# Queries of a hybrid decoder layer: projected in slabs by dimension, rotated in rows and sent through DRAM, instead of by item of four heads

## The chip, the cores and the metric

The kernel runs on one core of a Trainium2 chip. The metric is the time of one execution in microseconds (us) on the device. TensorE (PE in the profile, PEld its weight loads) does the matmuls; VectorE (DVE), ScalarE (ACT) and GpSimd (POOL) work element by element; SyncE (SP) issues all DMAs of this kernel. SBUF is the memory on the chip, with 128 partitions; matmul results arrive in PSUM, which has eight banks of 512 f32 a partition.

## What is computed

One decoder layer over 2048 tokens of width 1024, f32 in and out:

```python
h = rmsnorm(x, attn_norm)
z = h @ w_in              # [pool 1024 | q 16 heads x 64 | k, v 2 heads x 64 | two gates 1024 each]
q = partial_rope(rmsnorm(q, q_norm), positions) * 64 ** -0.5    # per head; the first 16 of 64 dimensions turn
k = partial_rope(rmsnorm(k, k_norm), positions)
b = swa_sink_attention(q, k, v, sinks)      # window of 128 tokens, 8 query heads to one key head
a = pool_mixer(u_pool)                      # causal means over 2, 4, 8, 16 tokens, a matrix a group
x = x + (g_pool * a + g_attn * b) @ w_out
h = rmsnorm(x, ffn_norm)
up = causal_depthwise_conv(h @ w_up)        # 2 x 2816 wide, 3 taps
x = x + (silu(gate) * val) @ w_down
```

`partial_rope` turns dimension d of the first eight with dimension d + 8: `x1 cos - x2 sin` and `x2 cos + x1 sin`. The norm divides by one number a head and token, so it can be applied after the scores' product: the kernel puts it into the scale of the exponential.

## The kernel before

It works through two chunks of 1024 tokens. Each chunk runs a mixer (projections, attention, pooling, gates), the output projection, the up projection and the down projection; the mixers are 0 to about 510 us and 1254 to about 1710 us of the profile. Each f32 operand is kept as a high and a low half in a reduced f32 format (fp32r), and a product is three matmuls: high by high, high by low, low by high. `mm3` issues them, so all projections have its line (L221 before, L225 after).

The program is written with a framework that allots tiles from pools of rotating buffers and fixes, before the run, one order of instructions for each engine; at run time each engine goes through its list in that order and waits on semaphores. So does SyncE with the DMAs, all of which `load` issues (L199 before, L203 after): a DMA that waits for its data holds up those behind it. PSUM tiles have the tags f, a and t, of two banks each, and s, one tile of two banks. SBUF tiles have tags too: U (the large ones), M, Q, R, F, and small ones.

A mixer starts with eight blocks of 128 tokens, in which keys and values are made (`keys_values`). Then come 32 items: four groups of four heads (q4 = 3, 2, 1, 0), and within each the eight blocks n of 128 tokens. An item before is:

- `queries` of the next item: 24 matmuls of 256 columns (four heads) into bank a; sums of squares in `head_rstd` (a ScalarE square, a VectorE reduction L649, an addition, a power on GpSimd L651); the rotation in `rope` (L629 to L633); and the high and low halves into a tile Q (casts L716, L718 on ScalarE, differences L717, L719 on VectorE).
- `transposes` (L725) of these through TensorE into bank t and by ScalarE into the layout of the scores, dimensions on partitions (L727). They stand at the end of the item's last filler.
- `probabilities` of the item before: four transposes (L774), a cast, a difference (L777) and two masks on GpSimd (L780, L783).
- `scores`: eight matmuls into s (L742), the window's mask (L751), the maximum (L756), four exponentials with the norm as scale (L763), and the division by the sum (L767).
- the fillers: units of 24 matmuls of 512 columns of the gates and of the pooled channels ("ga", "pu", "pg", `filler`), which give TensorE work while the other engines do the softmax. `fillers` shares them out: 8, 12, 12 and 8 to the groups, of eight items each, so 24 items of a chunk have one filler and 8 have two (chunk 0's first group also has units that fold the pooling matrices).
- `values` of the item before: four matmuls (L796) into bank a, added into the output of the gate (L803 to L806).

`first_fillers` puts some units between the blocks of keys and values. `weight_order` is the order in which weights are loaded; in chunk 0 they are split into halves and these kept in DRAM for chunk 1 (`made_`... in the DMAs).

## Time and profile before

| | |
|---|---|
| Time, three runs | 2460.86, 2460.86, 2464.63 us; median 2460.86 |
| The profiled execution | 2466.2 us, its span 2464.0 |
| TensorE's granted clock | 0.997 of full |
| HBM | 214 MB read, 87 MB written |
| DMA queue of SyncE | 94608 packets, 34.6% of 16 engines' span |

The profile is of one execution. Busy is the time in which an engine executes; the chain that ended last is followed back from the last instruction. A group of instructions is a line, an engine, an operation and its tiles with their shapes, with the count, the busy time in us and the mean ns of one; behind the second bar stands the engine's idle time before them and what ended it. In the timeline a row is a run of like instructions, from its first start. Matmuls overlap: the next one starts before the last has ended, so that the cost of a piece is the distance of two starts.

### The profile page before, as it was taken

Reading aid. Unit: us, or ns where it says so; the run is one execution under the profiler, and the core shown is the slowest. Engines: PE = TensorE matmul, PEld = TensorE weight load, DVE = VectorE, ACT = ScalarE, POOL = GpSimd, SP = SyncE. Lnnn points to the kernel's source line nnn. Section 1 sums busy time; section 2 is a strip of 40 time slices with the busy share of each in tenths; the row PEclk is TensorE's granted clock in tenths of the full one; section 3 lists DMA queues with packets and bytes.
Section 4 is the critical chain, followed back from the end, with each engine's and each line's share of the span. In section 5 each row is a group of like instructions: output and inputs, shape, how many; then the busy total and the mean of one; then the engine's idle time right before and its main releaser. Section 6 shows DMA issues by size and latency. Waiting matters only on the chain.

```text
span 2464.0 us, 32845 instructions
## 1 busy us (share of the span) xinstructions
PE 2426.2 (98%) x12224; PEld 2056.7 (83%) x12224; DVE 1928.2 (78%) x3452; ACT 1151.1 (47%) x2294; POOL 225.1 (9%) x217
## 2 busy tenths in 40 slices
PE   7999999999999999999999999999999999999999
PEld 7888888877888888888888888888888888887887
DVE  7778777877888887899846766678569888788994
ACT  6544444545555555543513443444445554554432
POOL 0122221200000000000002322222000000000000
PEclk9999999999999999999999999999999999999999
DMA  8613233257322233544332122211542222218321
GB/s 326 256 71 120 87 129 129 78 196 271 115 94 77 96 112 109 182 177 162 111 146 86 52 83 72 90 53 43 184 171 103 77 91 88 79 69 282 132 74 52
DMA packets 94767, 303.33 MB, mean 123 GB/s; under 512 B 10128, under 2 KB 12560, under 8 KB 83600
## 3 DMA queue, kind: packets, MB, share of 16 engines
q1 hardware_dynamic: 94608, 301.24, 34.6%
q8 instruction: 96, 1.57, 0.3%
q14 instruction: 63, 0.52, 0.1%
HBM read 214.17 MB, written 87.03 MB: 122 GB/s over the span
## 4 chain that ended last, share of the span: by engine, by line
PE 83%; DVE 10%; ACT 3%; issue 1%; DMA 1%; POOL 0%; SPq 0%; DVEq 0%; ACTq 0%
PE f L221 22%; PE f L1009 18%; PE t L1009 9%; PE a L221 6%; PE a L1009 4%; PE a L1299 4%; PE f L1299 4%; PE s L1299 4%; PE t L1299 4%; ACT Q L763 2%; PE s L742 1%; PE a L796 1%; DVE F L846 1%; PE t L774 1%; DVE U L206 1%
## 5 line engine op out<-in xcount | busy, mean ns | idle before, releaser
L221 PE MATMUL f<-U,U 128*128 128x512 f32 (+1 forms) x3168 | 735.8, 390 | 15.6 <-ACT U L205 8.3
L221 PEld LDWEIGHTS f<-U,U 128*128 128x128 f32 x3168 | 585.7, 190 | 136.9 <-DVE U L206 10.5
L1009 PE MATMUL f<-U,U 128*128 128x512 f32 x1512 | 359.8, 390 | 1.3 <-ACT Q L1027 1.3
L1009 PEld LDWEIGHTS f<-U,U 128*128 128x128 f32 x1512 | 283.5, 188 | 61.5 <-ACT Q L1027 2.2
L1075 DVE SCALAR_TENSOR_TENSOR M<-F,vc,M 128x1024 f32<-128x1024 f32 x176 | 225.0, 1282 | 129.3 <-ACT M L1072 129.0
L1009 PE MATMUL t<-U,U 128*128 128x512 f32 x1080 | 254.2, 389 | 0.0
L221 PE MATMUL a<-U,U 128*128 128x256 f32 x1920 | 247.1, 284 | 1.3 <-DVE M L500 1.3
L221 PEld LDWEIGHTS a<-U,U 128*128 128x128 f32 x1920 | 241.5, 192 | 6.7 <-ACT rB L567 1.5
L1009 PEld LDWEIGHTS t<-U,U 128*128 128x128 f32 x1080 | 202.8, 188 | 42.1
L763 ACT ACTIVATE Q<-s,st,r 128x128 f32<-128x128 f32 x256 | 114.2, 453 | 172.7 <-DVE st L758 166.6
L651 POOL TENSOR_TENSOR r<-r,mhalf 128x4 f32<-128x4 f32 (+1 forms) x80 | 76.4, 955 | 929.4 <-DVE r L650 897.5
L322 ACT CAST U<-R 128x1024 fp32r<-128x1024 f32 x120 | 125.5, 1053 | 65.9 <-DVE R L343 33.9
L323 DVE TENSOR_TENSOR U<-R,U 128x1024 fp32r<-128x1024 f32 x120 | 146.7, 1222 | 0.0
L1009 PE MATMUL a<-U,U 128*128 128x512 f32 x576 | 138.6, 390 | 0.0
L1009 PE MATMUL f<-U,M 128*128 128x512 f32 x504 | 124.3, 395 | 4.0 <-DVE F L1053 4.0
L1009 PEld LDWEIGHTS a<-U,U 128*128 128x128 f32 x576 | 108.0, 188 | 22.2
L1258 ACT CAST U<-U 128x1024 fp32r<-128x1024 f32 x74 | 77.2, 1051 | 86.1 <-PE a L1299 26.5
L1009 PEld LDWEIGHTS f<-U,M 128*128 128x128 f32 x504 | 95.8, 191 | 24.7 <-DVE F L1053 4.9
L1072 ACT ACTIVATE M<-F,vc 128x1024 f32<-128x1024 f32 x88 | 109.3, 1243 | 1.3
L1061 ACT COPY F<-f 128x512 f32<-128x512 f32 x42 | 24.6, 586 | 181.0 <-PE f L1009 181.0
L206 DVE TENSOR_TENSOR U<-R,U 128x512 fp32r<-128x512 f32 x142 | 93.9, 691 | 7.8 <-ACT U L205 7.2
L1259 DVE TENSOR_TENSOR U<-U,U 128x1024 fp32r<-128x1024 f32 x74 | 89.7, 1220 | 10.3 <-ACT U L1258 10.3
(259 smaller groups left out, 3892.8 us busy)
## 6 DMA issues: line engine op xcount, KB each, us to landing
R<-w_up SPq DMA_DIRECT2D x80, 512.0 KB, 3.3
actd<-M SPq DMA_DIRECT2D x44, 512.0 KB, 2.6
U<-w_down SPq DMA_DIRECT2D x88, 256.0 KB, 5.0
U<-actd SPq DMA_DIRECT2D x88, 256.0 KB, 5.2
R<-w_out SPq DMA_DIRECT2D x32, 512.0 KB, 4.7
U<-kept SPq DMA_DIRECT2D x12, 1024.0 KB, 7.5
made_ga<-U SPq DMA_DIRECT2D x8, 1024.0 KB, 7.9
made_q<-U SPq DMA_DIRECT2D x8, 1024.0 KB, 7.3
```

The source lines that it names most:

```text
L206: V.tensor_sub(lo[:, t], src[:, t], hi[:, t].bitcast(F32))
L221: nc.tensor.matmul(out, a, b, start=(i == 0), stop=(i == n - 1))
L322: A.copy(t[:, 0], raw)
L323: V.tensor_sub(t[:, 1], raw, t[:, 0].bitcast(F32))
L651: G.tensor_tensor(r, r, mhalf[:, 0:nh], op=ALU.pow)
L763: A.activation(pr[:, h, :], sc[:, h, 0:P], AF.Exp, bias=nm[:, h:h + 1], scale=it["rq"][:, h:h + 1], accum_out=rs[:, h:h + 1])
L1009: nc.tensor.matmul(bank, a[:, x, k, :], b[k // 2][:, y, k % 2, :], start=(first and i == 0), stop=(i == 11), skip_group_check=True)
L1072: A.activation(y, u[:, 2:], AF.Identity, bias=cw[:, 3, m:m + 1], scale=cw[:, 2, m:m + 1])
L1075: V.scalar_tensor_tensor(y, u[:, j:j + T], cw[:, j, m:m + 1], y, op0=ALU.mult, op1=ALU.add)
L1258: A.copy(hi, src)
L1259: V.tensor_sub(lo, src, hi.bitcast(F32))
L1299: nc.tensor.matmul(into[m], u[:, 0, c_], v[:, 1], start=(first and j == 0), stop=(k == n - 1 and j == 2), skip_group_check=True)
```

## The change

The queries are no longer made for each item but as units of the same kind as the fillers. The columns of `w_q` are reordered on the host so that a slab of 128 columns is 16 dimensions of eight heads. There are eight slabs j (0 to 3 for heads 0 to 7, 4 to 7 for heads 8 to 15), each in two halves n of 512 tokens. A unit `queries(c, j, n)` is 24 matmuls with 512 tokens moving, so that its result has dimensions and heads on partitions and tokens along the row. Even slabs go to bank f, odd ones to bank a, and behind the odd one the pair is finished: squares added; for the first pair of each eight heads, whose slabs hold the dimensions that turn together, `rotate` with sine and cosine as rows; high and low halves into tiles M; and eight writes of 64 partitions to DRAM (`qd`). The sums of squares over a head's dimensions are four f32 matmuls with a matrix of ones and zeros (`heads8`, L728). `rope_rows` makes the rows once a chunk from the tables that the keys use, by eight f32 matmuls with the identity (L491).

`load_queries` reads an item's queries from DRAM in the layout of the scores, 256 KB in one DMA, two items ahead. With that the items' `queries` and `transposes` are gone, and so are the queries' own tables.

The eight units of heads 8 to 15 stand between the blocks of keys and values (`first_fillers`), with the four "ga" units behind them; those of heads 0 to 7 are fillers of the first two groups, which have 12, 16, 12 and 8 fillers now: 16 items of a chunk have one filler and 16 have two. In an item scores come first; `probabilities` of the item before follow them, or stand behind the first filler where there are two. Tag Q has five buffers instead of four. Later lines have shifted: scores are L770, the window's mask L779, the division L795, probabilities L802 to L805, values L824.

```diff
+def queries_of(pair):
+
+    return [("q", 2 * pair + j, n) for n in range(2) for j in range(2)]
...
-    out = sum(ga[:1] + pg[:1] + fold + pu[:1] + ga[1:] + pg[1:] + pu[1:], [])
+    q = [queries_of(i)] if i < 2 else []
+    out = sum(ga[:1] + pg[:1] + q + fold + pu[:1] + ga[1:] + pg[1:] + pu[1:], [])
...
-        return [ga[0:1], [], ga[1:2], [], ga[2:3], [], ga[3:4], []]
+        return [q[0:1], q[1:2], q[2:3], q[3:4], q[4:5], q[5:6], q[6:7], q[7:8] + ga]
     fold = [("fold", j, 0) for j in FOLDS[FOLD_LEAD:FOLD_FIRST]]
-    return [[], fold[0:1], fold[1:2] + ga[0:1], fold[2:3] + ga[2:3] + fold[3:4], ga[1:2], [],
-            ga[3:4], []]
+    return [[], fold[0:1], fold[1:2] + q[0:2], fold[2:3] + fold[3:4], q[2:4], q[4:5], q[5:6],
+            q[6:8] + ga]
...
-    qp = pool("qp", 4)
+    qp = pool("qp", 5)
...
+    heads8 = cp.tile([P, 8], F32, "heads8")
+    V.reduce_sum(heads8, ident.rearrange("p (d h) -> p h d", h=8), axis=AX.X)
...
+    def rope_rows(c):
+
+        rows = up_.tile([P, 2, T], F32, "U")
+        pb = ps2.tile([P, T], F32, "s")
+        rb = mp.tile([P, NB, P], F32, "M")
+        V.tensor_copy(rb.rearrange("p b (i d h) -> p (b i) d h", i=2, d=8),
+                      ck[:, c * NB:(c + 1) * NB].rearrange("p b i d -> p (b i) d").unsqueeze(3)
+                      .to_broadcast([P, 2 * NB, 8, 8]))
+        for n in range(NB):
+            nc.tensor.matmul(pb[:, n * P:(n + 1) * P], rb[:, n, :], ident, start=True, stop=True)
+        for i in range(2):
+            A.copy(rows[0:64, i], pb[64 * i:64 * i + 64])
+        return rows
...
-    def queries(it):
+
+
+
+    qd = [[dp.tile([2, HD, 8, 512], F32, f"qd_{i}_{n}") for n in range(2)] for i in range(2)]
+    rq = cp.tile([P, 2, NB, 8], F32, "rq")
+    STARTS = ((0, 16), (8, 24), (32, 40), (48, 56))
+
+    def queries(c, j, n, hs, ta, st):
+        if n == 0:
+            st["q", j] = stream.get("q", j, later=later)
+        pq, c_ = project(hs, st["q", j], n, "fa"[j % 2])
+        sq = qp.tile([P, 512], F32, "Q")
+        A.square(sq, pq)
+        if j % 2 == 0:
+            st["even"] = pq, sq
+            return
+        pe, acc = st.pop("even")
+        V.tensor_add(acc, acc, sq)
+        if j % 4 == 1:
+            rotate(pe, pq, st["rows"], c_)
+        own, at = j // 4, j % 4
+        for i, src in ((at - 1, pe), (at, pq)):
+            t = mp.tile([P, 2, 512], F32R, "M")
+            A.copy(t[:, 0], src)
+            V.tensor_sub(t[:, 1], src, t[:, 0].bitcast(F32))
+            for e, r in enumerate(STARTS[i]):
+                load(qd[own][n][:, r:r + 8].rearrange("a d h t -> (d h) a t"),
+                     t[64 * e:64 * e + 64].bitcast(F32))
+        pn = ps.tile([P, 512], F32, "t")[:, 0:32].rearrange("p (b h) -> p b h", b=4)
+        for b in range(4):
+            nc.tensor.matmul(pn[:, b], acc[:, b * P:(b + 1) * P], heads8, start=True, stop=True)
+        r = rq[:, own, 4 * n:4 * n + 4]
+        if at == 1:
+            V.tensor_tensor(r, pn, e1[:, c, 4 * n:4 * n + 4].unsqueeze(2)
+                            .to_broadcast([P, 4, 8]), op=ALU.add)
+        else:
+            V.tensor_add(r, pn, r)
+            r = r.rearrange("p b h -> p (b h)")
+            G.tensor_tensor(r, r, mhalf, op=ALU.pow)
+
+    def rotate(a, b, rows, c_):
+
+        h = slice(0, 64)
+        c, s = rows[h, 0, c_], rows[h, 1, c_]
+        ga, gb = (vc[h, V_QG + i:V_QG + i + 1] for i in range(2))
+        t = mp.tile([P, 2, 512], F32, "M")
+        for i, (x, g) in enumerate(((a, ga), (b, gb))):
+            V.scalar_tensor_tensor(t[h, i], x[h], g, s, op0=ALU.mult, op1=ALU.mult)
+            V.scalar_tensor_tensor(x[h], x[h], g, c, op0=ALU.mult, op1=ALU.mult)
+        V.tensor_sub(a[h], a[h], t[h, 1])
+        V.tensor_add(b[h], b[h], t[h, 0])
+
+    def load_queries(it):
         c, q4, n = it["c"], it["q4"], it["n"]
-        hs, wq = it["hs"], it["wq"]
-        c_ = slice(n * P, (n + 1) * P)
-        bank = ps.tile([P, 512], F32, "a")
-        pq = bank[:, 0:256]
-        mm3(pq, [(hs[k][:, 0, c_], hs[k][:, 1, c_], wq[k // 4][:, 0, k % 4, :],
-                  wq[k // 4][:, 1, k % 4, :]) for k in range(KT)])
-        q = pq.rearrange("p (h d) -> p h d", h=4)
-        rq = head_rstd(bank, 4, c, n)
-        qr = sp.tile([P, 4, 16], F32, "qr", 1)
-        rope(qr, q, "q", c * NB + n, 4)
-        qs = qp.tile([P, 4, 2, HD], F32R, "Q")
-        A.copy(qs[:, :, 0, 16:HD], q[:, :, 16:HD])
-        V.tensor_sub(qs[:, :, 1, 16:HD], q[:, :, 16:HD], qs[:, :, 0, 16:HD].bitcast(F32))
-        A.copy(qs[:, :, 0, 0:16], qr)
-        V.tensor_sub(qs[:, :, 1, 0:16], qr, qs[:, :, 0, 0:16].bitcast(F32))
-        it.update(rq=rq, qs=qs)
-
-    def transposes(it):
-        pt = ps.tile([P, 4, P], F32R, "t")
-        for h in range(4):
-            nc.tensor.transpose(pt[:, h, :], it["qs"][:, h].rearrange("p a d -> p (a d)"), identr)
-        qT = qp.tile([P, 4, P], F32R, "Q")
-        A.copy(qT, pt.bitcast(F32))
-        it["qT"] = qT
+        it["qT"] = qp.tile([P, 4, P], F32R, "Q")
+        h, b = 4 * (q4 % 2), n % 4
+        load(it["qT"].bitcast(F32), qd[q4 // 2][n // 4][:, :, h:h + 4, b * P:(b + 1) * P]
+             .rearrange("a d h t -> (a d) h t"))
+        it["rq"] = rq[:, q4 // 2, n, h:h + 4]
...
         ta, st = {}, {}
+        if c > 0:
+            st["rows"] = rope_rows(c)
         for n in range(NB):
+            if c == 0 and n == 2:
+                st["rows"] = rope_rows(c)
...
-        wq = {3: stream.get("q", 3)}
-        items = [dict(c=c, q4=q4, n=n, hs=hs, kts=kts, vs=vs, ta=ta)
+        items = [dict(c=c, q4=q4, n=n, kts=kts, vs=vs, ta=ta)
                  for q4 in (3, 2, 1, 0) for n in range(NB)]
-        def head(i):
-            items[i]["wq"] = wq[items[i]["q4"]]
-            queries(items[i])
-
-        head(0)
-        transposes(items[0])
+        for it in items[0:2]:
+            load_queries(it)
         for i in range(len(items)):
             group, n = divmod(i, NB)
-            if n == NB - 3 and group < 3:
-                wq[2 - group] = stream.get("q", 2 - group)
-            if i + 1 < len(items):
-                head(i + 1)
-            if i > 0:
+            scores(items[i])
+            if i + 2 < len(items):
+                load_queries(items[i + 2])
+            fills = fillers(c, group)[n]
+            if i > 0 and len(fills) == 1:
                 probabilities(items[i - 1])
-            scores(items[i])
             run_later()
-            parts = fillers(c, group)[n]
-            for f in parts:
-                if f == parts[-1] and i + 1 < len(items):
-                    between.append(lambda: transposes(items[i + 1]))
+            for j, f in enumerate(fills):
+                if i > 0 and j == 1:
+                    probabilities(items[i - 1])
                 filler(*f, c, hs, ta, st)
             if i > 0:
                 values(items[i - 1])
...
-        "w_q": c(w[:, 1024:2048].reshape(2, 4, P, 4, 256).transpose(3, 0, 2, 1, 4)),
+        "w_q": slabs(w[:, 1024:2048][:, order]),
```

TensorE in the last group of chunk 1's mixer, one item; U_14668 and U_14670 are the queries' weights, U_11063 to U_11208 the normed tokens, t, a, s and f PSUM tiles. Before (the scores L742 and the filler follow):

```order
L725 MATMUL t_15712<-identr_136,Q_15643 128x128 x4
L796 MATMUL a_15721<-M_15656,U_11269 128x512 x2
L796 MATMUL a_15721<-M_15653,U_11269 128x512 x2
L221 MATMUL a_15732<-U_14668,U_11063 128x256 x3
L221 MATMUL a_15732<-U_14668,U_11085 128x256 x3
L221 MATMUL a_15732<-U_14668,U_11107 128x256 x3
L221 MATMUL a_15732<-U_14668,U_11130 128x256 x3
L221 MATMUL a_15732<-U_14670,U_11153 128x256 x3
L221 MATMUL a_15732<-U_14670,U_11170 128x256 x3
L221 MATMUL a_15732<-U_14670,U_11189 128x256 x3
L221 MATMUL a_15732<-U_14670,U_11208 128x256 x3
L774 MATMUL t_15773<-identr_136,Q_15675 128x128 x4
```

The changed kernel at the same place, up to the filler's first product and from its last one on to the next item's transposes:

```order
L824 MATMUL a_14015<-M_13984,U_10406 128x512 x2
L824 MATMUL a_14015<-M_13981,U_10406 128x512 x2
L770 MATMUL s_14026<-U_10404,Q_13896 128x256 x8
L802 MATMUL t_14052<-identr_136,Q_13966 128x128 x4
L225 MATMUL f_14067<-U_10200,U_13987 128x512 x3
```

```order
L225 MATMUL f_14067<-U_10345,U_13987 128x512 x3
L824 MATMUL a_14094<-M_14060,U_10406 128x512 x2
L824 MATMUL a_14094<-M_14057,U_10406 128x512 x2
L770 MATMUL s_14105<-U_10404,Q_13974 128x256 x8
L802 MATMUL t_14131<-identr_136,Q_14042 128x128 x4
```

The queries' products and their transposes are gone from the item, scores stand ahead of the transposes of the probabilities, and one filler is all that lies between those and the values.

VectorE at the same place; a_15721 and a_14094 are the values' bank, s the scores. Before:

```order
L806 SCALAR_TENSOR_TENSOR U_14067<-U_14067,Q_15726 128x2x128
L649 TENSOR_REDUCE r_15758<-a_15732 128x4
L629 TENSOR_TENSOR rope_15763<-a_15732,cq_181 128x64
L650 TENSOR_SCALAR r_15758<-r_15758,e_20_185 128x4
L631 TENSOR_TENSOR rope_15763<-a_15732,sq_182 128x4x8 x2
L777 TENSOR_TENSOR M_15778<-t_15773,M_15778 128x512
L633 TENSOR_TENSOR qr_15762<-rope_15763 128x64
L717 TENSOR_TENSOR Q_15768<-a_15732,Q_15768 128x4x48
L751 COPY_PREDICATED s_15784<-causal_140,s_15784 128x4x128
L719 TENSOR_TENSOR Q_15768<-qr_15762,Q_15768 128x4x16
L756 TENSOR_REDUCE st_15794<-s_15784 128x4
```

After:

```order
L832 TENSOR_TENSOR Q_14099<-a_14094,Q_14099 64x256
L779 COPY_PREDICATED s_14105<-causal_142,s_14105 128x4x128
L832 TENSOR_TENSOR Q_14099<-a_14094,Q_14099 64x256
L784 TENSOR_REDUCE st_14115<-s_14105 128x4
L834 SCALAR_TENSOR_TENSOR U_13003<-U_13003,Q_14099 128x2x128
L785 SCALAR_TENSOR_TENSOR st_14115<-st_14115,rq_193 128x4
L805 TENSOR_TENSOR M_14136<-t_14131,M_14136 128x512
L786 TENSOR_TENSOR st_14115<-st_14115,nsink_147 128x4
L905 SCALAR_TENSOR_TENSOR U_12089<-F_13750,vc_102,U_12089 128x512
```

The seven operations of the queries, six of them ahead of the window's mask, are gone, and the work on the values and the probabilities' low half now stands among that on the scores.

SyncE at the end of chunk 0's blocks of keys and values, in the changed kernel; R are raw weights, `made_` their halves kept for chunk 1, `qd` the queries in DRAM, Q an item's queries:

```order
L203 DMA qd_0_4_191<-M_1342 64x2x512 x2
L203 DMA R_1525<-w_q 128x1024
L203 DMA qd_0_4_191<-M_1347 64x2x512 x2
L203 DMA qd_1_5_192<-M_1449 64x2x512 x2
L203 DMA Q_1611<-qd_0_4_191 128x4x128
L203 DMA Q_1613<-qd_0_4_191 128x4x128
L203 DMA qd_1_5_192<-M_1454 64x2x512 x2
L203 DMA made_ga_0_13_1532<-U_1527 128x2048
```

Before, the same stretch of the queue is:

```order
L199 DMA R_1392<-w_ga 128x1024
L199 DMA made_ga_0_10_1394<-U_1269 128x2048
L199 DMA R_1630<-w_q 128x1024
L199 DMA R_1632<-w_q 128x1024
L199 DMA made_pu_0_11_1634<-U_1506 128x2048
L199 DMA R_1890<-wfold_84 128x1024
```

The query writes and the reads of the first items stand between weights and their copies; a write there waits for the difference on VectorE that ends its tile.

More of the change, by code (lines that the diff above doesn't have):

```diff
@@ L59 @@
 V_SK = V_CB + 44
-V_N = V_SK + NH
+V_QG = V_SK + NH
+V_N = V_QG + 2
 class Pool:
@@ L144, in weight_order @@
         out += [(kind, j) for parts in first_fillers(c) for kind, j, n in parts if n == 0]
-        out.append(("q", 3))
         for i in range(4):
-            for n, parts in enumerate(fillers(c, i)):
-                if n == NB - 3 and i < 3:
-                    out.append(("q", 2 - i))
-                out += [(kind, j) for kind, j, h in parts if h == 0]
+            out += [(kind, j) for parts in fillers(c, i) for kind, j, h in parts if h == 0]
         out += [("pg", ct) for ct in slabs_of(3)]
@@ L224, in block_kernel @@
     wfold = dp.tile([8, P, 8, P], F32, "wfold")
-    slabs = {"ga": w_ga, "pu": wfold, "pg": w_gp, "out": w_out, "fold": w_poolT}
+    slabs = {"ga": w_ga, "pu": wfold, "pg": w_gp, "out": w_out, "fold": w_poolT, "q": w_q}
     made = {}
@@ L241, in load_weights @@
             return None
-        if kind == "q":
-            srcs = [w_q[a[0], j] for j in range(2)]
-        elif kind == "up":
+        if kind == "up":
             srcs = [w_up[a[0]], w_up[FT + a[0]]]
@@ L270, in split_weights @@
             shape = [P, 2] + list(raw.shape)[1:]
-            if key[0] == "q":
-                out.append(up_.tile(shape, F32R, "U"))
-            else:
-                p, tag = (mp, "M") if out and key[1] not in FOLDS[:FOLD_LEAD] else (up_, "U")
-                out.append(p.tile(shape, F32R, tag))
+            p, tag = (mp, "M") if out and key[1] not in FOLDS[:FOLD_LEAD] else (up_, "U")
+            out.append(p.tile(shape, F32R, tag))
             hi, lo = out[-1][:, 0], out[-1][:, 1]
@@ L380, in block_kernel @@
     load(raw[1], w_poolT[lead[1]])
-    def load_gains():
-        t = qp.tile([P, 2, HD], F32, "Q")
-        load(t, qkn.rearrange("p (a d) -> p a d", a=2))
-        return t
-    gains = load_gains()
+    gains = qp.tile([P, 2, HD], F32, "Q")
+    load(gains, qkn.rearrange("p (a d) -> p a d", a=2))
     def load_rest():
@@ L477, in block_kernel, with rope_tables @@
     vcar = cp.tile([P, 2, P], F32R, "vcar")
-    cq = cp.tile([P, 16, 16], F32, "cq")
-    sq_ = cp.tile([P, 16, 16], F32, "sq")
     ck = cp.tile([P, 16, 2, 8], F32, "ck")
-    tabs["q"], tabs["k"] = (cq, sq_), ck
-    def rope_tables(chunk, gains):
+    tabs["k"] = ck
+    def rope_rows(c):
[10 more added lines that the diff above has]
+        return rows
+    def rope_tables(chunk):
         n, at = [P, NB, 8], slice(chunk * NB, (chunk + 1) * NB)
@@ L527, in rope_tables @@
             A.activation(dst, u, AF.Sin, scale=-tau)
-        for h in range(2):
-            own = gains[:, 0, 8 * h:8 * h + 8].unsqueeze(1).to_broadcast(n)
-            other = gains[:, 0, 8 - 8 * h:16 - 8 * h].unsqueeze(1).to_broadcast(n)
-            V.tensor_tensor(cq[:, at, 8 * h:8 * h + 8], cos, own, op=ALU.mult)
-            V.scalar_tensor_tensor(sq_[:, at, 8 * h:8 * h + 8], sin, 2.0 * h - 1.0, other,
-                                   op0=ALU.mult, op1=ALU.mult)
     r1 = cp.tile([P, NCH, NB], F32, "r1")
@@ L1339, in mixer @@
             block_b(n)
+            if n == 2 and c == 0:
+                turn(0)
             for f in fills:
                 filler(*f, c, hs, ta, st)
-            if n == 2 and c == 0:
-                turn(0)
             if n > 1 or n == c == 1:
@@ L1391, in block_kernel @@
     scaled()
-    rope_tables(0, gains)
+    rope_tables(0)
     for i, j in enumerate(FOLDS[:FOLD_LEAD]):
@@ L1433, in _layout @@
     w = np.asarray(w_in)[0]
+    starts = np.array([0, 16, 8, 24, 32, 40, 48, 56]).reshape(4, 2)
+    order = (np.arange(2)[:, None, None, None, None] * 512 + starts[None, :, :, None, None] +
+             np.arange(8)[:, None] + np.arange(8) * 64).reshape(-1)
     cw = np.asarray(conv_w)[0]
@@ L1437, in _layout @@
         [cols(cw[j]) for j in range(3)] +
-        [cols(conv_b), rows(sinks)], axis=1)
+        [cols(conv_b), rows(sinks)] +
+        [np.tile(np.repeat(np.asarray(q_norm).reshape(-1)[i:i + 8], 8), 2)[:, None] for i in (0, 8)],
+        axis=1)
     return {
```

37 lines of the change are left out of this document (15 added, 22 removed).

## The prediction

> **What bounds the kernel now.** I read the page first, for the bound of the whole; then TensorE's timeline in a quiet stretch of a mixer, for the price of each piece; then the waits there, the engines' load by stage, and the groups. From the page:
>
> ```profile
> span 2464.0 us, 32845 instructions
> PE 2426.2 (98%) x12224; PEld 2056.7 (83%) x12224; DVE 1928.2 (78%) x3452; ACT 1151.1 (47%) x2294; POOL 225.1 (9%) x217
> PE 83%; DVE 10%; ACT 3%; issue 1%; DMA 1%; POOL 0%; SPq 0%; DVEq 0%; ACTq 0%
> ```
>
> TensorE is busy for 98% of the span and the chain that ended last runs 83% through it. So a change is worth what it takes off TensorE's queue, plus or minus what it does to the 38 us in which TensorE stands. The profiled run took 2466.2 us, 5.3 above the median of 2460.86; durations come from it, the sum is taken off the median.
>
> One single-filler item of chunk 1, TensorE's timeline (start, duration, instruction, count, [idle before <- who ended it]); durations overlap, so I price a piece from its start to the next start:
>
> ```profile
> 1410.33 1.20 PE L742 MATMUL s<-U,Q 128*128 128x256 f32 x8
> 1411.37 11.07 PE L221 MATMUL f<-U,U 128*128 128x512 f32 x48
> ...
> 1426.44 0.60 PE L774 MATMUL t<-identr,Q 128*128 128x128 f32 x4
> 1426.80 1.20 PE L742 MATMUL s<-U,Q 128*128 128x256 f32 x8
> 1427.83 5.63 PE L221 MATMUL f<-U,U 128*128 128x512 f32 x24
> 1433.31 0.46 PE L725 MATMUL t<-identr,Q 128*128 128x128 f32 x4
> 1433.60 1.15 PE L796 MATMUL a<-M,U 128*128 128x512 f32 x4
> 1434.59 3.04 PE L221 MATMUL a<-U,U 128*128 128x256 f32 x24
> 1437.47 0.60 PE L774 MATMUL t<-identr,Q 128*128 128x128 f32 x4
> ```
>
> From it: probabilities' transposes 0.36 us, scores 1.03, a filler of 24 matmuls of 512 columns 5.48, queries' transposes 0.29, values 0.99, queries' 24 matmuls of 256 columns 2.88; an item is 11.03. TensorE never stands in these rows. Where it does stand in a mixer:
>
> ```profile
> 1409.95 0.63 PE L774 MATMUL t<-identr,Q 128*128 128x128 f32 x4 [1.10 <-DVE Q L767]
> ...
> 486.85 0.74 PE L742 MATMUL s<-U,Q 128*128 128x256 f32 x4 [1.79 <-ACT Q L727]
> ...
> 493.67 0.73 PE L796 MATMUL a<-M,U 128*128 128x512 f32 x2 [1.15 <-POOL M L783]
> ```
>
> Softmax, queries and masks each come late now and then, by 1 to 2 us. Busy time by stage (us, then PE, PEld, DVE, ACT, POOL busy, the granted clock, DMA's share, GB/s), for the start, for the last full 100 us of chunk 0's mixer and for a late one of chunk 1's:
>
> ```profile
> 0.00:100.00 100.00, 86.17 (x588) 80.03 (x589) 75.40 (x315) 60.93 (x144) 10.40 (x17) 0.98 0.82 307
> 400.00:500.00 100.00, 96.92 (x569) 84.33 (x569) 82.52 (x203) 51.12 (x151) 24.03 (x22) 1.00 0.22 76
> 1553.00:1653.00 100.00, 100.00 (x592) 88.22 (x591) 67.55 (x174) 39.82 (x129) 22.57 (x22) 1.00 0.20 74
> ```
>
> Chunk 0's items run with VectorE at 83% and 3 us of TensorE standing; chunk 1's at 68% and none. The clock is full in all but the first, so it enters no term.
>
> **The change part by part.** The groups that go or give a price (count | busy us, mean ns | idle before):
>
> ```profile
> L221 PE MATMUL a<-U,U 128*128 128x256 f32 x1920 | 247.1, 284 | 1.3 <-DVE M L500 1.3
> L725 PE MATMUL t<-identr,Q 128*128 128x128 f32 x256 | 29.7, 239 | 0.1
> L649 DVE TENSOR_REDUCE r<-a 128x4 f32<-128x256 f32 x64 | 27.2, 425 | 16.1 <-ACT a L647 14.6
> L717 DVE TENSOR_TENSOR Q<-a,Q 128x192 fp32r<-128x192 f32 x64 | 22.6, 353 | 0.8 <-ACT Q L716 0.7
> L719 DVE TENSOR_TENSOR Q<-qr,Q 128x64 fp32r<-128x64 f32 x64 | 37.7, 588 | 0.1
> L777 DVE TENSOR_TENSOR M<-t,M 128x512 fp32r<-128x512 f32 x64 | 43.7, 683 | 0.0
> ```
>
> 1. Projection. Of the 1920 short matmuls, 384 are keys and values; 1536, 64 items of 24, are queries and go: 64 x 2.88 = 184.3 us. In come 8 slabs x 2 halves x 2 chunks = 32 units of 24 at 512 columns: 32 x 5.48 = 175.4. Net -8.9, all on the path, since TensorE is the bound.
>    The Trainium skill, "TensorE: Matmul & The Clock Gate", section "Back-to-back issue gap", puts the warm gap of a matmul at N/2.4 + 2.5 ns, 109 ns for 256 columns and 216 for 512. By that two halves cost 2.5 ns more than a whole, an estimate of 768 x 2.5 ns = 1.9 us saved, and the sum would come out 7 us higher. The rows above, 2.88/24 = 120 ns and 5.48/24 = 228 ns, differ from it, and make that surplus 11.7 ns.
> 2. Queries' transposes: 256 = 64 x 4 go, 64 x 0.29 = -18.6.
> 3. Norm sums. The sums of squares over a head's dimensions, a VectorE reduction before, become four plain f32 matmuls (128x128 by 8 columns) behind each pair of units, 16 groups, 64 in all. The nearest rows are the f32 sums of the feed-forward's norm, where one matmul leaves two records, and the spreading by an identity, four matmuls in eight records:
>
> ```profile
> 1823.91 0.28 PE L554 MATMUL a<-one,F 128*128 128x1 f32 x2
> ...
> 1825.39 0.36 PE L554 MATMUL a<-one,M 128*128 128x1 f32 x2
> 1825.62 3.01 PE L1009 MATMUL f<-U,U 128*128 128x512 f32 x12
> 1828.47 1.05 PE L565 MATMUL s<-identr,M 128*128 128x128 f32 x8
> 1829.28 2.98 PE L1009 MATMUL a<-U,U 128*128 128x512 f32 x12
> ```
>
>    Eight in 1.71 us (1823.91 to 1825.62), 0.214 each: 64 x 0.214 = +13.7.
> 4. Rope rows: sine and cosine turned into rows once a chunk, 8 spreads each: 0.81 us for four (1828.47 to 1829.28), 16 of them, +3.2.
>    TensorE's queue: -8.9 - 18.6 + 13.7 + 3.2 = -10.6.
> 5. VectorE, ScalarE, GpSimd. Each item loses L649, L717, L719 (425 + 353 + 588 = 1366 ns) and four smaller operations: over 87 us of 64 items' VectorE time. Each unit gains an operation of 128x512 (like L777, 0.68), every second one an addition of such a size, and every second pair six on 64 rows: at most 32 x 0.68 + 16 x 0.68 + 8 x 6 x 0.68 = 65. GpSimd's powers go from 64 to 4 wider ones. VectorE gets lighter by 22 us at least. None of it is on the path by itself; the margins of point 7 are.
> 6. The start. In chunk 0 four pairs of query units, two of them rotated, run between the key blocks, their banks held by the rotation and the casts, while VectorE builds the first halves of everything, and behind the query writes on SP's queue stand the x rows and the weights. TensorE already loses 13.8 us in that first 100. Nearest row for a bank or table late there:
>
> ```profile
> 33.84 1.19 PE L221 MATMUL a<-U,U 128*128 128x256 f32 x8 [1.30 <-DVE M L500]
> ```
>
>    Two such waits would be 2.6; the floor is 0 (the gate units that stood there wait for weights too), the ceiling about 12, nearly as much again as is lost there now. I take the two waits, +2.5.
> 7. The items. Scores now lead, and probabilities of item i-1 follow scores of i, or come after its first filler where it has two. The 8 query units that move ahead and the 8 left as fillers make 12, 16, 12, 8 fillers for the four groups in place of 8, 12, 12, 8, so 16 items a chunk have a single one (24 before). Such an item shrinks from 11.03 to 1.03 + 0.36 + 5.48 + 0.99 = 7.86 us. From scores' end to the transposes that need their softmax there are now 0.36 + 5.48 + 0.99 + 1.03 = 7.86 less a little overlap, and from transposes to values 5.84. What that chain takes now, in the item whose scores end at 1411.37:
>
> ```profile
> 1413.72 0.69 DVE L751 COPY_PREDICATED s<-causal,s 128x512 f32<-128x512 uint8 x1
> ...
> 1418.72 0.69 DVE L767 TENSOR_TENSOR Q<-Q,st 128x512 f32<-128x512 f32 x1
> ```
>
> ```profile
> 1414.90 1.09 POOL L783 TENSOR_SCALAR_AFFINE_SELECT M<-M 128x1024 fp32r<-128x1024 f32 x1
> ```
>
>    L751 came 2.35 us after scores' end, behind the queries' operations that leave, and L767 ended at 1419.41, 8.0 us after; without that delay about 6. The masks ended at 1415.99, 6.0 after the transposes began (1409.95); their second half is needed 0.5 into values, at 6.3. Softmax has some 1.5 us of room and the masks 0.3, where before both had 3 or more. The price is bounded below by losing most of the present waits (three of 1.1 to 1.8 are shown; some -8), above by a wait of 0.6 us in each of the 32 short items, +20. I take +2: the short items stand a little more in chunk 0, where VectorE is fullest, the long ones less.
> 8. The way through DRAM. Every pair of units issues eight writes of 256 KB, every item one read, all on SP.
>
> ```profile
> x2d<-M SPq DMA_DIRECT2D x32, 256.0 KB, 4.0
> U<-x2d SPq DMA_DIRECT2D x8, 1024.0 KB, 5.8
> ```
>
>    A write lands in 4.0 us and a larger read back in 5.8: 10 us, against four gate fillers (22 us) between the last query unit and the first scores and two items (15 us or more) after that. Cost 0, covered by those; if the reads stuck behind weight loads on SP, one such trip a group, 8 x 10 = 80 at worst, would show.
>
> Sum: -10.6 + 2.5 + 2 + 0 = -6.1, so 2460.9 - 6.1 = 2454.8.
>
> **The rivals.**
> A. As summed: 2454.8, between 2450 and 2459 by the looseness of points 6 and 7.
> B. The items' waits fall too. For it: VectorE's load drops by 22 us or more, and L751 stood behind operations that go. Against: chunk 1 has hardly a wait left to lose. -10.6 + 2.5 - 8 = -16.1: 2444.8.
> C. The start eats the gain: with 10 lost there, -10.6 + 10 + 2 = +1.4, 2462.3. For it: VectorE and ScalarE are at 75 and 61% there, in a stretch where TensorE waits on them; against, the key blocks leave other work to run.
> D. Slower: in the 32 short items softmax or masks are longer than what covers them. One mechanism, each period set by VectorE's row of operations instead of TensorE's. It decides from (10.6 - 2.5)/32 = 0.25 us an item; at 0.6 it is -10.6 + 2.5 + 19 = +11, 2472, at 1.1 it is +27, 2488. For it: 6.0 us of masks under a cover of 6.3, and 8 us of softmax under 7.9. Against: what made the softmax late is what leaves.
> E. A whole costs as much as two halves, so that the 2.88 is a matter of the place: units at 5.76, the 8.9 gone, 2463.7. The skill's gap rule of point 1 is nearly that (2461.8). Against: both rows stand in one item, at full clock.
> F. The layout by DRAM comes late, the change not delivering what the scores need: half of the groups 10 us late is +40 - 6, about 2495. Against: twice the cover.
>
> **How the numbers follow.** No change is what lies within 0.2%, 4.9 us, about what a measurement of this kernel can tell: 2455.9 to 2465.8. A 0.42 (0.30 of it under 2455.9), B 0.17, C 0.17, D 0.17, E 0.04, F 0.03. Faster 0.30 + 0.17 = 0.47; the same 0.12 + 0.17 + 0.04, and a little of D's foot, 0.35; slower 0.18. The range leaves out the lowest of B, D above 0.6 us an item, and F: 2443 to 2473. A's own is 2450 to 2459.
>
> **What would show it.** TensorE's groups: 768 more f32r matmuls of 512 columns at 228 ns apart, no L725's successor, 64 short f32 sums at about 0.21 us; TensorE's busy time less by 10 us or so. In the last 80 us of each mixer items of 7.9 us: waits of values on GpSimd's second mask or of transposes on the softmax of more than 0.25 us each would bring D. Waits of query units on a bank between 30 and 100 us above 2.5 would bring C. A wait of scores on a DMA at all would bring F. I am wrong if the sums run far from 0.21 us, or if VectorE in the short items is too full to keep the 7.9.

## The result, and the profile after

The changed kernel takes 2481.78 us (median of 2475.48 to 2482.72), the kernel before 2461.57 beside it: the ratio is 1.0072, with a 95% interval of 1.0059 to 1.0084. It is slower, by about 15 to 20 us, where 6 us faster was forecast, and above the range.

The profiled execution is the fastest of the four, at a granted clock of 0.999; the others ran at 0.996 and 0.997. Later, executions of the kernel before at 0.999 took 2460.0 to 2463.0 us, so at one clock the change costs about 14 us; that is what two traces can explain, and the rest of the 20 stands beside a lower clock of the other three executions, for which no run here shows a cause. From the page of the changed kernel:

```profile
span 2473.8 us, 30606 instructions
PE 2416.9 (98%) x11360; PEld 2003.3 (81%) x11360; DVE 1901.9 (77%) x3047; ACT 1101.3 (45%) x2106; POOL 226.5 (9%) x161
PE 80%; DVE 12%; ACT 3%; DMA 2%; issue 2%; POOL 1%; SPq 0%; DVEq 0%; ACTq 0%; POOLq 0%
```

TensorE is busy for 9.3 us less and the span is 9.8 longer, so TensorE waits. From the view of its waits (engine, line and who was waited for; us in total, times, longest) these belong to the items, the changed kernel first:

```profile
PE s L770 <- ACT Q L791: 9.7, 10, 1.7
PE a L824 <- POOL M L811: 8.7, 16, 1.4
PE a L824 <- POOL M L808: 4.1, 7, 1.0
PE t L728 <- DVE Q L715: 1.9, 2, 1.4
PE a L824 <- DVE st L785: 1.1, 1, 1.1
PE t L802 <- DVE Q L795: 0.9, 1, 0.9
```

```profile
PE t L774 <- DVE Q L767: 3.5, 4, 1.2
PE s L742 <- ACT Q L727: 3.1, 2, 1.8
PE a L796 <- POOL M L783: 2.1, 2, 1.2
```

Scores wait for the exponentials of the item before, which free their bank, and values for GpSimd's two masks. (A seventh row of the changed kernel, values on L787, has 0.2 us; and one of the two waits of L728, 0.5 us, lies at the start, at 64 us.) The whole view adds up to 51.4 us at 57 places, before to 33.0 at 30. A wait costs more than its length. This is TensorE in chunk 1 of the changed kernel, an item of one filler and the scores of the next, with the values of the item before it at the top:

```profile
1600.21 1.07 PE L824 MATMUL a<-M,U 128*128 128x512 f32 x4
1601.11 1.11 PE L770 MATMUL s<-U,Q 128*128 128x256 f32 x8
1602.07 0.60 PE L802 MATMUL t<-identr,Q 128*128 128x128 f32 x4
1602.42 5.71 PE L225 MATMUL f<-U,U 128*128 128x512 f32 x24
1607.97 1.07 PE L824 MATMUL a<-M,U 128*128 128x512 f32 x4
1610.02 1.21 PE L770 MATMUL s<-U,Q 128*128 128x256 f32 x8 [0.98 <-ACT Q L791]
1611.07 5.63 PE L225 MATMUL f<-U,U 128*128 128x512 f32 x24
```

Where no wait follows, values take 0.90 and scores 0.96 from start to start, as in the first two rows; further down they take 2.05 and 1.05, 1.24 more for a wait of 0.98. I call the 0.26 on top the refill; over many waits it comes to an estimated 0.2 to 0.3 us each (last section). So 27 more waits of 18.4 us cost 24 to 27. A queue that is shorter by the sum's 10.6 leaves 13 to 16, by the 7 to 10 that the runs show (below) 14 to 20: the 14 us at one clock lie at the lower end.

Why scores waited there is on VectorE, from the scores' end at 1602.2:

```profile
1602.62 0.68 DVE L779 COPY_PREDICATED s<-causal,s 128x512 f32<-128x512 uint8 x1
1603.39 0.69 DVE L805 TENSOR_TENSOR M<-t,M 128x512 fp32r<-128x512 f32 x1
...
1604.58 0.69 DVE L784 TENSOR_REDUCE st<-s 128x4 f32<-128x512 f32 x1
1605.30 0.42 DVE L834 SCALAR_TENSOR_TENSOR U<-U,Q 128x256 f32<-128x256 f32 x1
1605.64 1.05 DVE L785 SCALAR_TENSOR_TENSOR st<-st,rq 128x4 f32<-128x4 f32 x1
1606.61 1.23 DVE L874 TENSOR_TENSOR F<-F 128x1036 f32<-128x1036 f32 x1
1607.76 0.15 DVE L786 TENSOR_TENSOR st<-st,nsink 128x4 f32<-128x4 f32 x1
...
1610.41 0.69 DVE L795 TENSOR_TENSOR Q<-Q,st 128x512 f32<-128x512 f32 x1
```

```profile
1604.16 1.09 POOL L808 TENSOR_SCALAR_AFFINE_SELECT M<-M 128x1024 fp32r<-128x1024 f32 x1 [5.05 <-DVE M L805]
1605.32 1.36 POOL L811 TENSOR_SCALAR_AFFINE_SELECT M<-M 128x1024 fp32r<-128x1024 f32 x1
```

The maximum's product L785, on four numbers a partition, takes 1.05 us in place of 0.16 and ends at 1606.69, when the second mask ends (1606.68). That mask in turn took 1.36 in place of 1.09, having begun under L834. And between L785 and L786, for which the exponentials wait, VectorE's fixed order holds an operation of 1.23 us for the pooling (L874). So the first exponential began 5.8 us after the scores' end, and the last ended 7.7 after it:

```profile
1608.01 0.46 ACT L791 ACTIVATE Q<-s,st,rq 128x128 f32<-128x128 f32 x1 [4.26 <-DVE st L786]
...
1609.42 0.45 ACT L791 ACTIVATE Q<-s,st,rq 128x128 f32<-128x128 f32 x1
```

The next scores could have begun 0.90 us after the values, at 1608.87, that is 6.7 after the scores' end; they began when the last exponential had freed the bank. In the short item of the kernel before whose scores end at 1428.0 (1426.80 in the prediction's rows), the last exponential ended 5.3 us after that and the next scores stood 9.8 after it:

```profile
1432.85 0.46 ACT L763 ACTIVATE Q<-s,st,r 128x128 f32<-128x128 f32 x1
```

```profile
1437.82 1.20 PE L742 MATMUL s<-U,Q 128*128 128x256 f32 x8
```

### The profile page after: what moved, and what is told of

The parts are those of the page before. It is cut to its first block, busy times and chain, and to the rows that moved or that the text cites. A ratio compares the mean times of both kernels' runs of the same rounds, so it can differ in the third digit from the quotient of the medians.

```text
span 2473.8 us, 30606 instructions
## 1 busy us (share of the span) xinstructions
PE 2416.9 (98%) x11360; PEld 2003.3 (81%) x11360; DVE 1901.9 (77%) x3047; ACT 1101.3 (45%) x2106; POOL 226.5 (9%) x161
## 4 chain that ended last, share of the span: by engine, by line
PE 80%; DVE 12%; ACT 3%; DMA 2%; issue 2%; POOL 1%; SPq 0%; DVEq 0%; ACTq 0%; POOLq 0%
PE f L225 22%; PE f L1037 18%; PE t L1037 9%; PE a L225 4%; PE a L1037 4%; PE a L1327 4%; PE f L1327 4%; PE s L1327 4%; PE t L1327 4%; PE s L770 1%; ACT Q L791 1%; DVE F L874 1%; DVE U L210 1%; PE a L824 1%; DVE Q L832 1%
## 5 line engine op out<-in xcount | busy, mean ns | idle before, releaser
L225 PE MATMUL f<-U,U 128*128 128x512 f32 (+1 forms) x3552 | 832.6, 390 | 16.3 <-DVE U L210 7.6
L225 PEld LDWEIGHTS f<-U,U 128*128 128x128 f32 x3552 | 654.6, 189 | 151.0 <-DVE U L210 11.4
L1037 PEld LDWEIGHTS f<-U,U 128*128 128x128 f32 x1512 | 283.3, 188 | 61.5 <-ACT Q L1055 2.2
L791 ACT ACTIVATE Q<-s,st,rq 128x128 f32<-128x128 f32 x256 | 114.2, 452 | 157.9 <-DVE st L786 145.6
L225 PE MATMUL a<-U,U 128*128 128x256 f32 (+1 forms) x768 | 142.3, 339 | 2.1 <-DVE M L510 1.3
L808 POOL TENSOR_SCALAR_AFFINE_SELECT M<-M 128x1024 fp32r<-128x1024 f32 x64 | 84.7, 1323 | 569.7 <-DVE M L805 391.6
L225 PEld LDWEIGHTS a<-U,U 128*128 128x128 f32 x768 | 119.5, 189 | 17.7 <-ACT rB L570 1.5
L1037 PEld LDWEIGHTS a<-U,U 128*128 128x128 f32 x576 | 108.0, 188 | 22.3
L1287 DVE TENSOR_TENSOR U<-U,U 128x1024 fp32r<-128x1024 f32 x74 | 89.5, 1218 | 10.6 <-ACT U L1286 10.6
```

The costliest lines, as they stand in the source:

```text
L225: nc.tensor.matmul(out, a, b, start=(i == 0), stop=(i == n - 1))
L791: A.activation(pr[:, h, :], sc[:, h, 0:P], AF.Exp, bias=nm[:, h:h + 1], scale=it["rq"][:, h:h + 1], accum_out=rs[:, h:h + 1])
L808: G.affine_select(cur.rearrange("p a h q -> p (a h) q"), pin, pattern=[[0, 8], [1, P]], base=0, channel_multiplier=-1, compare_op=ALU.is_g ...
L1037: nc.tensor.matmul(bank, a[:, x, k, :], b[k // 2][:, y, k % 2, :], start=(first and i == 0), stop=(i == 11), skip_group_check=True)
L1287: V.tensor_sub(lo, src, hi.bitcast(F32))
```

## The experiments

The two theories at the start: the covers in the items are too short (T), or the loss lies outside the items. A cover is the TensorE work between the start of a chain on the other engines and the matmuls that need its end. Each experiment is an edit of the changed kernel unless it says otherwise.

### No masks: e1_no_masks

```diff
-        cur = mp.tile([P, 2, 4, P], F32R, "M")
-        G.affine_select(cur..., compare_op=ALU.is_ge, fill=0.0)
-        if b > 0:
-            G.affine_select(pa..., compare_op=ALU.is_gt, fill=0.0)
-        it.update(cur=cur, prev=pa)
+        it.update(cur=pa, prev=pa)
```

> The changed kernel with both of GpSimd's masks on the probabilities left out (values take the unmasked halves). Theory, covers too short: the changed kernel's loss is in TensorE's waits inside the items, of values on the masks (12.8 us idle at 23 places) and of scores on the exponentials (9.7 us at 10), each with a further 0.27 us in which the pipeline refills; without masks the first go (-19 us), and the softmax's small operations no longer stand behind GpSimd, so some of the second too: 2455 to 2466, values waiting nowhere. Rival, the loss lies outside the items (the start, the way through DRAM, the clock): under 6 us faster than the changed kernel's 2481.8.

2446.58 us, 0.9933 of the kernel before (0.9919 to 0.9948): 35 us less than the changed kernel by the medians, 27 by the spans of the two profiled executions (2446.5 and 2473.8, at 0.998 and 0.999), where T expected 16 to 27. So by the medians T's size was too small; its rival's, under 6, is out. The waits in the items that are left:

```profile
PE s L770 <- ACT Q L791: 3.6, 4, 1.5
PE t L802 <- DVE Q L795: 0.8, 1, 0.8
PE t L728 <- DVE Q L715: 0.8, 2, 0.5
```

So the waits on the exponentials were mostly the masks' doing too. VectorE's groups say how (count | busy us, mean ns), the changed kernel and then the one without masks:

```profile
L787 DVE TENSOR_TENSOR st<-st,nsink 128x4 f32<-128x4 f32 x64 | 23.3, 364 | 1.1
L785 DVE SCALAR_TENSOR_TENSOR st<-st,rq 128x4 f32<-128x4 f32 x64 | 17.5, 273 | 0.3
```

```profile
L787 DVE TENSOR_TENSOR st<-st,nsink 128x4 f32<-128x4 f32 x64 | 10.1, 158 | 1.1
L785 DVE SCALAR_TENSOR_TENSOR st<-st,rq 128x4 f32<-128x4 f32 x64 | 9.9, 155 | 0.3
```

What the masks cost lies in the items, so the theory that the loss lies outside them is out. Whether the kernel before loses as much to its masks, the next runs say.

### The kernel before without masks: e5_before_no_masks, e9_before_no_masks

The same edit in the kernel before.

> The kernel before with both masks on the probabilities left out, as e1_no_masks left them out of the changed kernel. Theory: the masks are late only in the changed kernel, where 5.9 us cover them in place of 7.2 or more; before, they cost 2.1 us of waits and what they hold up on VectorE, mostly off the path: 2454 to 2461. Then the two kernels without masks differ by TensorE's queue (-10.6) and little else, 8 to 15 us. Rival, GpSimd's masks cost the kernel before as much as the changed one: 2432 to 2445, and without masks the change saves nothing.

One of its four executions, the profiled one, took 12100 us, for which no run shows a cause; the others took 2444.87 to 2452.03. So the kernel was run again.

> The same kernel as e5_before_no_masks, since the profile of that one fell on an execution of 12100 us. Theory: the kernel before has 11.8 us of waits in its items at 15 places, with some 0.29 us of refilling each 16 us, and nearly all of them come from the masks, on the values directly and through VectorE's small operations that stand behind GpSimd: with no masks its items wait under 3 us in all, 2445 to 2450. Rival, it wins without its waits going: TensorE's queue itself gets shorter, waits of the items still 8 us or more.

2446.51 us, 0.9933 (0.9916 to 0.9949). T's figure for the kernel before, 2454 or more, was wrong: it too loses 17 us to the masks by the medians, some 14 at one clock (these executions ran at 0.999 to 1.000, those of the kernel before beside them at 0.998). The rival's 2432 to 2445 was wrong as well, but not its claim that without masks the change saves nothing; and e9's own theory, 2445 to 2450 with under 3 us of waits in the items, held. In its trace no wait of an item on the softmax, the queries or the masks is left: L774, L742 and the values do not appear in the view of waits, which holds 24.1 us at 20 places. Two groups of VectorE get shorter with it, L757 from 332 to 160 ns and L719 from 588 to 217: they had stood behind the masks. And without masks the change is worth nothing, 2446.58 against 2446.51. The trace of the changed kernel has 30.0 us at 26 places there, 5.9 more (4.4 of them on the exponentials and the softmax); with the refills that is 7 us, at the same span, 2446.5 and 2446.6. TensorE's queue is about 7 us shorter, up to 10 with the clocks of the two executions (0.998 and 0.999), and the new waits take it all.

### A longer cover: e11_longer_short

```diff
                 filler(*f, c, hs, ta, st)
+            if len(fills) == 1:
+                more = ps.tile([P, 512], F32, "f")
+                mm3(more, [(hs[k][:, 0, 0:P], hs[k][:, 1, 0:P], hs[k][:, 0, 0:512],
+                            hs[k][:, 1, 0:512]) for k in range(4)])
             if i > 0:
                 values(items[i - 1])
```

> The changed kernel with half a filler more, 12 matmuls of 512 columns whose result nothing reads, in each of the 32 items that have a single one, between that filler and the values: 32 x 2.74 = 87.7 us more on TensorE. Theory, covers too short: masks, exponentials and softmax all get 2.74 us more there, more than the largest wait (1.7), so nearly all of the items' 27.4 us of waits at 39 places and their refills (39 x 0.29) go: 2481.8 + 87.7 - 35 = 2534, 2528 to 2544. Rival, VectorE's order and its stand-offs with GpSimd set the waits however long the cover: the waits stay, 2562 to 2572.

2533.72 us, 1.0288 (1.0273 to 1.0304), as T had it: some 87 us of matmuls (2.72 in each item) cost 52 by the medians, 58 by the spans of the two profiled executions (2531.5 at a clock of 1.000, 2473.8 at 0.999). All its waits are 31.9 us at 29 places, 19.5 less at 28 fewer; those of the items:

```profile
PE a L824 <- POOL M L811: 2.3, 4, 0.7
PE t L728 <- DVE Q L715: 1.8, 2, 1.4
PE a L824 <- POOL M L808: 1.3, 2, 0.9
PE s L770 <- ACT Q L791: 0.2, 1, 0.2
```

VectorE's order and its stand-offs with GpSimd are the same (L785 takes 258 ns in the mean and L787 404, in the changed kernel 273 and 364); with 2.7 us more in the short items they cost nearly nothing. That is T's cause shown: the covers are too short for chains that have not changed.

### The order in an item: e2_probs_next, e7_probs_lead, e3_values_next

e2 puts the probabilities right behind the next scores in all items, e7 ahead of the scores as before, and e3 moves the values too, in the last two groups:

```diff
 # e2 (scores lead)
-            if i > 0 and len(fills) == 1:
+            if i > 0:
                 probabilities(items[i - 1])
...
 # e7: the two lines ahead of scores(items[i])
...
 # e3, behind e2's
+            if i > 2 * NB:
+                values(items[i - 2])
             run_later()
...
-            if i > 0:
+            if 0 < i < 2 * NB:
                 values(items[i - 1])
+        values(items[-2])
```

> The changed kernel with the probabilities' transposes right behind the next item's scores in items of two fillers as well, so that both fillers, not one, lie between them and the values. Theory, covers too short: the waits of values on the masks in those items go (about half of 12.8 us and of 23 refills of 0.27), 2470 to 2476; those in items of one filler stay. Rival, the masks are late because VectorE's queue is late as such: the waits stay or become waits of the transposes on the softmax, 2479 to 2485.

2476.43 us, 1.0054 (1.0039 to 1.0069), between T's range and the rival's. The waits on the masks went from 12.8 to 11.6 us only: those left are nearly all in items of one filler, and items of two had held about 2. At the clock 0.999 it took 2474.89, the changed kernel 2475.48. What I had said of the long items was wrong; they cost little.

> The changed kernel with the order in an item as before: probabilities of the item before, then scores, then the fillers, then values. Theory: in items of one filler the masks get 6.9 us in place of 5.9, and in those of two 12, but the softmax has 6.5 in place of 7.8, just its shortest: the waits move to the transposes, 2470 to 2485. Rival, that scores lead is what costs: 2452 to 2462.

2477.99 us, 1.0065 (1.0050 to 1.0080). The masks are in time and the softmax is late instead:

```profile
PE s L770 <- ACT Q L791: 15.5, 17, 3.0
PE t L802 <- DVE Q L795: 6.0, 7, 3.2
PE a L824 <- POOL M L811: 1.4, 3, 0.8
```

That scores lead is not what costs.

> As e2_probs_next, and in the last two groups of four heads the values of item i-2 stand behind the probabilities of item i-1, ahead of the fillers, so that the masks there have an item (some 7.8 us) instead of 5.9, and the values' VectorE work comes after the start of the next softmax instead of ahead of it. Theory: no waits of values on masks left but a few (-19 against the changed kernel), waits of scores on the exponentials about as now (9.7) or fewer: 2458 to 2466. Rival, the softmax is what limits the short items, and a mask in time only moves the wait to the scores: 2468 to 2478, with over 15 us of waits on the exponentials.

2482.46 us, 1.0075 (1.0060 to 1.0090). The rival's waits came, masks 5.8 us in place of 12.8 and the exponentials 19.7 in place of 9.7; the time is 4 us above its range. In an item of 7.8 us each of the three orders only chose which chain is late.

### The stand-off: e4_max_in_psum

```diff
-        V.reduce_max(mx, sc[:, :, 0:P], axis=AX.X)
-        V.scalar_tensor_tensor(nm, mx, -1.0, it["rq"], op0=ALU.mult, op1=ALU.mult)
-        V.tensor_tensor(nm, nm, nsink[:, sk], op=ALU.min)
-        V.tensor_sub(es, nm, nsink[:, sk])
+        mx, n0, n1 = (sc[:, :, P + j] for j in range(3))
+        V.reduce_max(mx, sc[:, :, 0:P], axis=AX.X)
+        V.scalar_tensor_tensor(n0, mx, -1.0, it["rq"], op0=ALU.mult, op1=ALU.mult)
+        V.tensor_tensor(nm, n0, nsink[:, sk], op=ALU.min)
+        V.tensor_tensor(n1, n0, nsink[:, sk], op=ALU.min)
+        V.tensor_sub(es, n1, nsink[:, sk])
```

> The changed kernel with the maximum and its product with the norm in PSUM (the free half of the scores' bank), one more small operation, so that none of the softmax's operations ahead of the exponentials reads two operands from SBUF. Theory: these small operations took 273, 212 and 364 ns (332, 160, 161 before) because some of them stood for 1 us until a mask on GpSimd ended; now about 160 to 200 each, and the masks 1.14 us instead of 1.32 and 1.30: 3 to 8 us faster than the changed kernel. Rival, they stood behind something else in VectorE's queue: same durations, no gain, 0 to 4 us slower by the added operation.

2479.65 us, 1.0070 (1.0053 to 1.0087): no gain that can be told. The mechanism is right and the price was wrong. With one operand in PSUM the operations take 154 to 162 ns in the mean (L786 never more than 171), and the waits on the exponentials fall from 9.7 to 5.2; but the masks, expected shorter, got longer, and the values wait more:

```profile
PE a L826 <- POOL M L813: 13.7, 19, 1.5
PE s L770 <- ACT Q L793: 5.2, 9, 0.9
```

```profile
L786 DVE SCALAR_TENSOR_TENSOR s<-s,rq 128x4 f32<-128x4 f32 x64 | 10.4, 162 | 0.3
L813 POOL TENSOR_SCALAR_AFFINE_SELECT M<-M 128x1024 fp32r<-128x1024 f32 x60 | 82.8, 1380 | 4.1
```

The trace shows two things more that worked against a gain. In the item at the same place the stand-off passed to the next operation in VectorE's order, the pooling's addition of two SBUF operands, which also stands ahead of the exponentials: beside a second mask from 1607.58 to 1608.95 it took 2.05 us in place of 1.23.

```profile
1607.99 2.05 DVE L876 TENSOR_TENSOR F<-F 128x1036 f32<-128x1036 f32 x1
```

And the edit changed ScalarE's fixed order too: the small exponential (L790) now leads the four large ones and waits for L789, one more pooling operation later, so that the first large one began 7.1 us after the scores' end there (1604.48 to 1611.59). How much each cost, no run separates; e8 has the same order on ScalarE.

### One mask: e6_one_mask, e8_one_mask_psum, e10_before_one_mask, e12_later_queries

The masked probabilities of the two blocks add up to the unmasked ones. So values can multiply the unmasked by the earlier block's v and the masked by the difference of the two v, which is made once a chunk, high and low halves; the second mask goes.

```diff
...
-        todo = [(vs[:, n, g, :], it["cur"])]
+        todo = [(vs[:, 0, g, :], it["cur"])]
         if c * NB + n > 0:
-            todo.append((vs[:, n - 1, g, :] if n > 0 else vcar[:, g, :], it["prev"]))
+            todo = [(vs[:, n - 1, g, :] if n > 0 else vcar[:, g, :], it["prev"]),
+                    (it["vd"][:, n, g, :], it["cur"])]
...
```

> The changed kernel with one mask instead of two: values multiply the unmasked probabilities by the earlier block's values and the masked ones by the difference of the two blocks' values, made once a chunk (eight operations on VectorE and two on ScalarE more a chunk). The unmasked products go first. Theory: the masks' chain is 1.2 us shorter and is needed 0.45 us later, which is more than nearly all of the waits on it (largest 1.4), and GpSimd blocks VectorE half as long: 2450 to 2460. Rival, VectorE is what is full: it gets 8 us more work a chunk and the scores' waits grow, 2470 to 2482.

2455.24 us, 0.9974 (0.9964 to 0.9985), as expected. Values wait once, 0.5 us:

```profile
PE s L770 <- ACT Q L791: 5.7, 5, 2.0
PE t L802 <- DVE Q L795: 3.6, 7, 1.3
PE a L836 <- POOL M L810: 0.5, 1, 0.5
```

> e6_one_mask and the maximum in PSUM of e4_max_in_psum. Theory: with one mask the exponentials' operations are no longer held by GpSimd and the masks have room, so what the one frees the other does not take: 2 to 6 us faster than e6_one_mask. Rival, with one mask there is nothing left to free: within 2 us of e6_one_mask.

2454.34 us, 0.9966 (0.9952 to 0.9980), within the rival's 2 us of e6.

> The kernel before with one mask, as e6_one_mask has it. Theory: its waits shrink as those of the changed kernel did, but there is less to win: 2449 to 2456, and with one mask the change is worth 0 to 5 us in either direction. Rival, the kernel before has room for both masks, so it only gets the added work: 2460 to 2468, and the changed kernel with one mask stays 5 us or more ahead.

2455.09 us, 0.9968 (0.9956 to 0.9979). With one mask the kernel before is 8 us faster and as fast as the changed kernel with one mask (2455.24 and 2454.34): there, too, the change is worth nothing in either direction. So it loses only where two masks stand in the chain of the short items.

The start, on top of e8, in `first_fillers`:

```diff
-    return [[], fold[0:1], fold[1:2] + q[0:2], fold[2:3] + fold[3:4], q[2:4], q[4:5], q[5:6],
+    return [[], fold[0:1], fold[1:2], fold[2:3] + fold[3:4], q[0:2], q[2:4], q[4:6],
             q[6:8] + ga]
```

> e8_one_mask_psum, and in chunk 0 the first two query units two blocks of keys and values later (behind block 4 instead of 2) and those behind them closer together, away from the first 70 us in which VectorE builds the first halves. Theory: the changed kernel's start loses 2.2 us of waits more than before (16.0 against 13.8, four waits at 50 to 64 us, 2.0 us) with a refill each, and these go: 1 to 3 us faster than e8_one_mask_psum. Rival, TensorE lacks other work there, since the weights and the first tokens are late whatever runs: the waits go to other instructions, within 1 us of e8_one_mask_psum.

2454.68 us, 0.9964 (0.9952 to 0.9976), not to be told from e8. The waits between 40 and 70 us, 3.2 us in e8 and 3.3 here, fell on other instructions, as the rival said. All four kernels with one mask beat both kernels of this case, the kernel before by 7 to 9 us, and e10 does so without the change.

## Why the prediction was wrong, point by point

Points 1 to 4, TensorE's queue, held. Norm sums: a group of four took 0.91 us, where 0.86 were taken (0.214 each); eight spreads took 1.80 (1260.32 to 1262.12), where 1.62 were taken.

```profile
1300.40 1.06 PE L728 MATMUL t<-heads,Q 128*128 128x8 f32 x8
1301.31 0.51 PE L692 MATMUL t<-identr,Q 128*128 128x128 f32 x4
```

A unit of 24 took 5.47 us (1611.07 to 1616.54), or 5.55 where values follow it (the row at 1602.42). The gap rule of the Trainium skill ("TensorE: Matmul & The Clock Gate", section "Back-to-back issue gap"), by which two halves cost hardly more than a whole, has no support in these rows either: 5.47 against twice 2.88. A short item without a wait took 7.76 (1601.11 to 1607.97, and 0.90 for the values) where 7.86 were foreseen. With these prices the sum gives a queue 7.1 to 9.7 us shorter, and e9 against e1 gives 7 to 10, where 10.6 were forecast.

Point 6, the start, was of the right size: TensorE's busy time in the first 100 us fell by 2.4, with about 2.2 us more of waits.

```profile
0.00:100.00 100.00, 83.80 (x558) 76.21 (x559) 75.44 (x281) 58.13 (x132) 7.59 (x14) 1.00 0.86 316
1553.00:1653.00 100.00, 95.44 (x476) 79.44 (x475) 69.63 (x138) 32.83 (x108) 20.76 (x18) 1.00 0.36 129
```

Point 8 held: no scores waited on a DMA. (A pair of units issues four writes of 256 KB, not eight, 64 in all; and in point 5 GpSimd has 8 wide powers, not 4. Neither enters the sum.)

Point 7 is the step that failed, and rival D, given 0.17, is what came, in the main. Its term was +2 and measures 24 to 27: by the rows above the items' waits grew from 8.7 us at 8 places to 26.6 at 38, by 17.9, and each of 30 more places has its refill (waits on weights, elsewhere in the mixers, fell by 1.0 at 5 fewer places, some 2 with the refills). Over the 32 short items that is about 0.8 us each (some 2 us of it lies in items of two fillers), where D decided from 0.25; at 0.8 D's sum gives 2478. D's mechanism came only in part: the chains are longer than their covers, but VectorE is not what sets every period. The second window above shows it: in 1553 to 1653 us TensorE had been busy throughout, and now stands for 4.6 us with VectorE at 70%. Four things in the working were wrong. First, I set single margins, 1.5 us for the softmax and 0.3 for the masks, against a typical item and took the sum of misses as +2; a margin of 0.3 on a chain that varied by over 1 us should have put the value near the upper end of -8 to +20, and that end was still too low. Second, I looked at one end of the softmax only, the transposes, 7.86 us after the scores. The next scores need the bank that the last exponential frees, and they come 6.7 us after the scores, in place of 9.8: this cover is in no term, and its waits are 9.7 us at ten places, where the transposes waited once, for 0.9. Third, I took the softmax to be 6 us once the queries' operations were gone; in the item above it took 8.9 (L795 ends at 1611.1). Other work took their place in VectorE's order (the values' addition, the probabilities' low half, the pooling), and the small operations stood behind GpSimd. The group with 332 ns for L757 against 160 for L758, and L719 with 588 ns for 64 columns, showed that stand-off before, as e9 confirms; I read neither as one. Fourth, no price for the refill was in the sum.

Rival B's premise came true and its gain did not: VectorE is busy for 26 us less (1928.2 to 1901.9), but not where the short items are: in the window from 1553 us it is at 69.6%, before at 67.6%.

## What to carry to other kernels

Work moved out of a loop shortens the loop, and with it every cover in it: divide each chain (here transposes, cast, difference and two masks, 6 us) by the new period before counting what TensorE saves, and list what each chain releases: here also the scores' bank. Where the margin is a few tenths of a microsecond and the chains cross engines in a fixed order, a new order of the pieces may only move the wait, as three did here; what helped was to take an operation off the chain. And to test such a theory, lengthening the cover by dead work is as good as removing the chain: here both told the same story.
